# Four layers on one core: a block transpose on VectorE, value products in one series, four column groups, and a normalisation that waits

## The chip, the core and the metric

The kernel runs on one core of a Trainium2 chip. TensorE (PE) multiplies, VectorE (DVE), ScalarE (ACT) and GpSimd (POOL) work element by element, SyncE (SP) issues the DMAs. The metric is the device time of one execution in microseconds. In the profile, PEld is TensorE's weight load and PEclk the clock that TensorE was granted, as a share of full speed.

## The reference

Four sub-layers act on `x` (1024 positions, width 1024, fp32). Each one normalises, mixes, gates and projects back:

```python
h = rmsnorm(x, norm_g[i]) * (1.0 + scale) + shift          # scale, shift, gate = c @ ada_w[i] + ada_b[i]
# i = 0, 3: HGRN2, 8 heads of 128
q, f_pre, i_, z = jnp.split(h @ w_in, 4, axis=-1)           # in outline
f = lb + (1 - lb) * sigmoid(f_pre); k = (1 - lb) * sigmoid(-f_pre); q = silu(q)
S_t = f_t * S_{t-1} + k_t v_t^T;  o_t = q_t S_t             # chunkwise in the code
y = (rmsnorm(o, onorm_g) * silu(z)) @ w_out
# i = 1: 16 query heads of 64 over 4 key heads, window of 128, sinks, rotary, q and k normalised per head
s = einsum(q, k over this block of 128 and the one before) * 64 ** -0.5
y = (softmax with sink(s masked) @ v * silu(z)) @ w_out
# i = 2: gated DeltaNet, 16 value heads of 128 over 8 key heads, causal convolution of 4 taps on q, k, v
X = triangular_solve(A + eye, rhs, unit_diagonal=True)      # per chunk; then a scan over the chunks
y = (rmsnorm(o, onorm_g) * silu(z)) @ w_out
x = x + gate * y
```

## The kernel before

The 1024 positions are worked in two halves of `HT` = 512. Every fp32 projection is split into a high and a low part and done as three products of 128x512 per 128 rows of the contraction (`mm3`, L204 to L206). A weight tile comes by DMA into `w_raw` (L177), ACT rounds it to `w_hi` (L179), DVE subtracts to `w_lo` (L180).

One program order is given by the Python text, and a scheduler turns it into one instruction list per engine by priorities. `weave` steps several generators together by the costs they yield and their totals; `high_priority`, `early` and `burst` (4000) move what is issued inside them forward; `tied` is a burst whose later products may not be parted from the first. Each engine then runs its own list in order, so an instruction that waits holds up all that is behind it on that engine.

*Normalisation* (`norm_apply`, L496 to L506): for each of 8 slices of 128 rows, DVE makes `n_t`, ACT makes `hhi`, DVE makes `hlo`. At the end of a layer both halves of the next layer's input are made there.

*HGRN2* (`hgrn2`, layers 0 and 3): eight heads. While head h is mixed (`mix`), the next head's projections run beside it as filler. In `mix`, levels of growing size fill an attention matrix: each level builds operands `hg_X` (L1061 to L1065, ACT and DVE) and multiplies 32-wide column groups of TensorE (L1040); the last level (L1087) has 12 products of 96, 64 and 32 columns in three column groups. At the end of a head's half, `o_ps` is normalised into `hg_tmp` (L1132), four TensorE transposes turn it into `ot_ps` (L1136), DVE multiplies by the gate `hg_zs` (L1139), and seven of eight heads store to `od` in DRAM.

*Attention* (`swa`, layer 1): K and V of half 0 early, then of half 1, then queries and gates. In `mix`, per block of 128 queries: scores, softmax, then for each of two key blocks four transposes (`pt_ps`, L1368), an ACT copy (`sw_pth`) and two products with the values (`pv_ps`, L1374), the second block's added to the first's.

*Gated DeltaNet* (`gdn`, layer 2): a convolution's eviction takes `gd_xs` (L644) and `gd_tb` (L648) from `proj_ps` on ACT and adds three taps on DVE (L650); `inverse` solves the triangles in steps whose products `z_ps` (L828 among them) are evicted by ACT and DVE. The DVE block transpose (`gd_of`, L859) is already used there, on 128x512 as 32x32 blocks, with stores to `od` of 64 KB (L862).

Of the kernel before, what the change touches and what calls it, by code (L numbers as in the profile page):

```python
# [20 lines left out]
P = 128  # L21
# [9 lines left out]
NB = {"n_acc": 1, "n_sq": 2, "n_t": 2}  # L31
# [52 lines left out]
class Trunk:  # L84
    def __init__(self, ctx, tc, ins):
# [11 lines left out]
        self.od = [self.dram.tile([D * (1 + n), T], F32, name=f"od{n}") for n in range(2)]  # L97
        self.zd = self.dram.tile([2 * D, T], F32, name="zd")
        self.hhi, self.hlo = [None, None], [None, None]
        self.x = [None, None]  # L100
        self.oo, self.pre = {}, {}
# [364 lines left out]
    def norm(self, i, hf):  # L466
        self.norm_apply(i, hf, self.norm_stats(hf))

# [27 lines left out]
    def norm_apply(self, i, hf, rb):  # L496
        nc = self.nc
        x = self.x[hf]
        self.hhi[hf], self.hlo[hf] = self.hslot("hhi"), self.hslot("hlo")
        hhi, hlo = self.hhi[hf], self.hlo[hf]  # L500
        for k in range(KT):
            t = self.np.tile([P, HT], F32, name="n_t", tag="n_t", bufs=NB["n_t"])
            G, S = self.gcol[:, i, k:k + 1], self.shift(i, k)
            nc.vector.scalar_tensor_tensor(t, x[:, k, :], G, rb, ALU.mult, ALU.mult)
            nc.scalar.activation(hhi[:, k, :], t, AF.Identity, bias=S)
            nc.vector.scalar_tensor_tensor(hlo[:, k, :], t, S, hhi[:, k, :].bitcast(F32), ALU.add, ALU.subtract)  # L506

# [29 lines left out]
    def gdn(self, i, side):  # L537
# [98 lines left out]
        def conv(dd, hf, ps, ct, out):  # L636
# [12 lines left out]
            for j in (2, 1, 0):  # L649
                nc.vector.scalar_tensor_tensor(y, xs[:, j:j + HT], w(j), y, ALU.mult, ALU.add)  # L650
# [81 lines left out]
        def inverse(u, dd):  # L732
# [79 lines left out]
            nc.scalar.copy(Z[R[1], :, 0:32], za[R[1]])  # L812
            nc.vector.tensor_copy(Z[R[3], :, 0:32], zb[R[3]])
# [8 lines left out]
            nc.scalar.copy(Z[R[1], :, 0:32], za[R[1]])  # L822
            nc.vector.tensor_copy(uv[R[2], :, R[3]], zb[R[2]])
            nc.vector.tensor_copy(uv[R[0], :, R[1]], za[R[0]])
# [7 lines left out]
            nc.scalar.copy(Z[up, 0:8], z[up])  # L832
            nc.vector.tensor_copy(Z[up, 8:16], z[lo])
# [4 lines left out]
            nc.scalar.copy(uv[lo, 0:8, up], z[lo])  # L838
            nc.vector.tensor_copy(uv[lo, 8:16, up], z[up])
# [25 lines left out]
        def scan(u, dd):  # L865
# [3 lines left out]
            for n in range(C):  # L869
# [50 lines left out]
        self.early(proj_kq(0, ds[0], ((0,),)), EV)  # L920
# [4 lines left out]
              (chain(proj_z(0, ds[0], (1,)), proj_v(0, ds[0]), proj_z(1, ds[1]), proj_kq(1, ds[1])), 72800, 0, 1, 0))  # L925
# [30 lines left out]
    def hgrn2(self, i, side):  # L956
# [7 lines left out]
        bufs = {"X": 1, "q": 3, "f": 3, "kg": 3, "qf": 3, "tmp": 3, "v": 3, "zs": 3, "kht": 1, "k0": 2}  # L964
# [60 lines left out]

        def mix(h, d, halves=(0, 1)):
            S = d.get("S")
            for hf in halves:
# [22 lines left out]
                for l in (1, 3, 5):  # L1051
# [9 lines left out]
                    nc.scalar.copy(xv[:, :, 0:3, :], qv[:, :, 1:4, :])  # L1061
                    nc.vector.tensor_tensor(xv[:, :, 3:5, :], qv[:, :, 2:4, :], bc(1, 3, 2), ALU.mult)
                    nc.vector.tensor_tensor(xv[:, :, nx - 1, :], xv[:, :, 4, :], bc(1, 2, 1)[:, :, 0, :], ALU.mult)
# [14 lines left out]
                    else:  # L1078
# [4 lines left out]
                        with self.burst():  # L1083
                          for c in range(NC):
                            for g in range(3):
                                gs = slice(g * 32, (g + 1) * 32)
                                nc.tensor.matmul(pl[gs, c, g + 1:, :], kg[:, c * P + g * 32:c * P + (g + 1) * 32], xv[:, c, g::3 if g == 0 else 4 - g, :][:, :3 - g, :] if g < 2 else xv[:, c, 2:3, :], start=True, stop=True)  # L1087
                        for g in range(3):
                            gs = slice(g * 32, (g + 1) * 32)
                            nc.scalar.copy(at[gs, :, (g + 1) * 32:], pl[gs, :, g + 1:, :].rearrange("p c b t -> p c (b t)"))  # L1090
                        yield 900
                    for b in (2, 1):
# [17 lines left out]
                sqj = tl("tmp")  # L1110
                for c in range(NC):
# [15 lines left out]
                    nc.scalar.activation(sqj[:, cs], po[:, cs], AF.Square, accum_out=ssq[:, c:c + 1])  # L1127
# [3 lines left out]
                on = tl("tmp")  # L1131
                nc.vector.tensor_tensor(on.rearrange("p (c t) -> p c t", c=NC), po.rearrange("p (c t) -> p c t", c=NC), r[:, :, None].to_broadcast([P, NC, P]), ALU.mult)  # L1132
                pt = self.psum("tr", "ot_ps", 1)
                for c in range(NC):
                    cs = slice(c * P, (c + 1) * P)
                    nc.tensor.transpose(pt[:, cs], on[:, cs], self.ident)  # L1136
                yield 436
                of = tl("tmp")
                nc.vector.tensor_tensor(of, pt, d["zs", hf], ALU.mult)  # L1139
# [10 lines left out]
        ds = [dict() for _ in range(H)]  # L1150
        gv = proj_v(0)
# [67 lines left out]
    def swa(self, i, side):  # L1219
# [33 lines left out]
        def rotate(tp, ps, cg, sg, out):  # L1253
# [7 lines left out]
            nc.vector.tensor_tensor(b4[:, :, :, 32:64], p4[:, :, :, 0:32], bc(sg, slice(32, 64)), ALU.mult)  # L1261
            nc.vector.tensor_tensor(out, a, b, ALU.add)

# [228 lines left out]
```

## Time and profile before

| | |
|---|---|
| runs shown | 2697.25, 2688.8, 2688.89 us; median 2688.89 us |
| profiled execution | 2695.95 us, span 2694.2 us, mean granted clock 0.992 |
| stages, from the start | setup 0 to 76, HGRN2 to 640, attention to 1115, gated DeltaNet to 2130, HGRN2 to the end |
| busy share | PE 97%, PEld 78%, DVE 75%, ACT 47%, POOL 5% |
| chain that ended last | PE 71%, DVE 17%, DMA 5%, ACT 3% |

The busy time of an engine says how full it is over the whole span. A wait of TensorE is listed with the tile and the line that waited, then the engine, tile and line that released it. In the timeline, an instruction's start to the next one's start is what it cost, since matmuls overlap at their ends and the durations shown overlap too.

### The profile page before, as it was taken

The page shows a single profiled execution, that of the slowest core. Times are in us where ns is not written, and L with a number is a line of the kernel's source. Part 1 is how long each engine was busy: PE and PEld are TensorE (multiplying, and loading weights), DVE is VectorE, ACT ScalarE, POOL GpSimd, SP SyncE. Part 2 cuts the span into 40 slices and gives each one's busy share as a digit, 9 for nine tenths or more (in the row PEclk, how much of TensorE's full clock was granted, in tenths as well). Part 3 has the DMA queues.
Part 4 walks back from the last instruction along what each step waited for, and adds up shares of the span by engine and source line. Part 5 has one row for each costly group of instructions (what it writes and reads, how often), then busy time and mean ns, then how long its engine had stood idle before and what let it go on. Part 6 is the DMA issues. An engine that isn't in the chain of part 4 may idle for free.

```text
span 2694.2 us, 51458 instructions
## 1 busy us (share of the span) xinstructions
PE 2609.7 (97%) x18927; PEld 2102.4 (78%) x18927; DVE 2010.2 (75%) x5619; ACT 1272.9 (47%) x3268; POOL 136.7 (5%) x352
## 2 busy tenths in 40 slices
PE   8999999999999999999999999999999999999998
PEld 4878878778878777677877777777788878787877
DVE  6776766788687877777988888989876766656575
ACT  4333333444454655454556556666644433333342
POOL 0000100000000000001001101100000000000000
PEclk9999999999999999999999999999999999999999
DMA  6332222344223252333343333333584221111133
GB/s 241 92 93 84 68 79 72 110 137 157 59 87 103 75 158 91 114 98 84 102 115 99 96 105 100 94 97 82 179 254 132 71 60 37 56 51 43 49 118 115
DMA packets 361490, 273.29 MB, mean 101 GB/s; under 512 B 70499, under 2 KB 294166, under 8 KB 361238
## 3 DMA queue, kind: packets, MB, share of 16 engines
q1 hardware_dynamic: 360950, 268.96, 33.9%
q8 instruction: 149, 2.44, 0.4%
q14 instruction: 103, 0.84, 0.1%
q0 software_dynamic: 288, 1.05, 0.1%
HBM read 224.77 MB, written 45.15 MB: 100 GB/s over the span
## 4 chain that ended last, share of the span: by engine, by line
PE 71%; DVE 17%; DMA 5%; ACT 3%; issue 3%; SPq 1%; POOL 0%; DVEq 0%; ACTq 0%; POOLq 0%
PE proj_ps L206 10%; PE proj_ps L205 9%; PE proj_ps L204 9%; PE outp_ps L204 5%; PE outp_ps L205 5%; PE outp_ps L206 5%; DMA ada_w<-in_ada_w_dram 3%; PE projt_ps L204 3%; PE projt_ps L206 3%; PE projt_ps L205 3%; DVE w_lo L180 2%; DVE gd_tb L650 2%; PE pv_ps L1374 1%; DVE ada_acc L413 1%; PE w_ps L890 1%
## 5 line engine op out<-in xcount | busy, mean ns | idle before, releaser
L204 PE MATMUL proj_ps<-hhi,w_hi 128*128 128x512 f32 x1664 | 675.8, 406 | 6.1 <-ACT gd_tb L648 5.9
L206 PE MATMUL proj_ps<-hhi,w_lo 128*128 128x512 f32 x1664 | 679.9, 409 | 0.0
L205 PE MATMUL proj_ps<-hlo,w_hi 128*128 128x512 f32 x1664 | 671.2, 403 | 0.0
L204 PEld LDWEIGHTS proj_ps<-hhi,w_hi 128*128 128x128 f32 x1664 | 315.3, 190 | 59.4 <-ACT gd_tb L648 6.3
L205 PEld LDWEIGHTS proj_ps<-hlo,w_hi 128*128 128x128 f32 x1664 | 314.7, 189 | 59.0 <-issue 2.4
L206 PEld LDWEIGHTS proj_ps<-hhi,w_lo 128*128 128x128 f32 x1664 | 315.0, 189 | 56.1 <-issue 1.0
L179 ACT CAST w_hi<-w_raw 128x512 fp32r<-128x512 f32 x332 | 202.0, 611 | 303.3 <-PE proj_ps L205 188.1
L180 DVE TENSOR_TENSOR w_lo<-w_raw,w_hi 128x512 fp32r<-128x512 f32 x332 | 223.1, 674 | 155.2 <-ACT w_hi L179 129.1
L205 PE MATMUL projt_ps<-w_lo,hhi 128*128 128x256 f32 x896 | 258.7, 291 | 4.7 <-DVE w_lo L180 4.7
L204 PE MATMUL projt_ps<-w_hi,hhi 128*128 128x256 f32 x896 | 257.8, 290 | 0.6 <-ACT w_hi L179 0.6
L206 PE MATMUL projt_ps<-w_hi,hlo 128*128 128x256 f32 x896 | 256.8, 290 | 0.0
L204 PE MATMUL outp_ps<-o_hi,w_hi 128*128 128x512 f32 x576 | 229.2, 400 | 4.7 <-ACT o_hi L1200 3.4
L205 PE MATMUL outp_ps<-o_lo,w_hi 128*128 128x512 f32 x576 | 229.4, 399 | 0.0
L206 PE MATMUL outp_ps<-o_hi,w_lo 128*128 128x512 f32 x576 | 226.8, 396 | 0.7 <-DVE w_lo L183 0.7
L205 PEld LDWEIGHTS projt_ps<-w_lo,hhi 128*128 128x128 f32 x896 | 171.1, 192 | 8.1 <-DVE w_lo L180 6.0
L204 PEld LDWEIGHTS projt_ps<-w_hi,hhi 128*128 128x128 f32 x896 | 171.1, 192 | 3.7 <-ACT w_hi L179 1.0
L206 PEld LDWEIGHTS projt_ps<-w_hi,hlo 128*128 128x128 f32 x896 | 170.8, 192 | 2.4 <-issue 1.0
L650 DVE SCALAR_TENSOR_TENSOR gd_tb<-gd_xs,taps,gd_tb 128x512 f32<-128x512 f32 x192 | 145.2, 756 | 28.3 <-ACT gd_tb L648 19.7
L182 ACT ACTIVATE w_hi<-w_raw,par 128x512 fp32r<-128x512 f32 (+1 forms) x136 | 94.3, 698 | 137.0 <-PE outp_ps L205 89.2
L204 PEld LDWEIGHTS outp_ps<-o_hi,w_hi 128*128 128x128 f32 x576 | 108.8, 189 | 29.1 <-ACT o_hi L1200 4.9
L413 DVE SCALAR_TENSOR_TENSOR ada_acc<-ada_w,par,ada_acc 128x512 f32<-128x512 f32 x140 | 104.8, 749 | 33.4 <-DMA ada_w<-in_ada_w_dram 32.5
L206 PEld LDWEIGHTS outp_ps<-o_hi,w_lo 128*128 128x128 f32 x576 | 108.7, 189 | 23.5 <-DVE w_lo L183 1.3
(398 smaller groups left out, 4894.8 us busy)
## 6 DMA issues: line engine op xcount, KB each, us to landing
ada_w<-in_ada_w_dram SPq DMA_DIRECT2D x160, 256.0 KB, 2.8
w_raw<-in_hg_in_w_dram SPq DMA_DIRECT2D x136, 256.0 KB, 2.8
w_raw<-in_gd_in_w_dram SPq DMA_DIRECT2D x108, 256.0 KB, 3.0
o_in<-od SPq DMA_DIRECT2D x72, 256.0 KB, 3.2
w_raw<-in_gd_out_w_dram SPq DMA_DIRECT2D x64, 256.0 KB, 2.9
w_raw<-in_sw_in_w_dram SPq DMA_DIRECT2D x48, 256.0 KB, 2.9
w_raw<-in_hg_out_w_dram SPq DMA_DIRECT2D x40, 256.0 KB, 2.8
ada_w<-in_ada_w_dram SPq DMA_DIRECT2D x8, 1024.0 KB, 9.2
```

What stands on the lines that cost most here:

```text
L179: nc.scalar.copy(hi, raw)
L180: nc.vector.tensor_tensor(lo, raw, hi.bitcast(F32), ALU.subtract)
L182: nc.scalar.activation(hi, raw, AF.Copy, scale=scale)
L204: mm(out, a[0], b[0], start=start, stop=False)
L205: mm(out, a[0], b[1], start=False, stop=False)
L206: mm(out, a[1], b[0], start=False, stop=stop)
L413: self.nc.vector.scalar_tensor_tensor(acc, w, c, acc, ALU.mult, ALU.add)
L650: nc.vector.scalar_tensor_tensor(y, xs[:, j:j + HT], w(j), y, ALU.mult, ALU.add)
L890: nc.tensor.matmul(po[:, hd[a]], dd["u"][a, hf][:, cs], rhs, start=True, stop=True)
L1374: nc.tensor.matmul(po[a * 64:(a + 1) * 64], vg[:, n + 1 - nkb + b, :], p4[:, :, a, :], start=b == 0, stop=b == nkb - 1)
```

## The change

1. `norm_apply` is a generator over its 8 slices, with `n_t` in PSUM. The second half's normalisation of the next layer is kept in `self.last`. HGRN2 and attention drain it at their start; gated DeltaNet takes four slices after each convolution's last tap, with `proj_z(1)` of half 0 now in the early part, and the total of the first weave goes from 72800 to 62400.
2. In `inverse`, evictions of z are in `burst`; in HGRN2, the operands `hg_X` too.
3. HGRN2's last level is 16 products of 32, 64, 64 and 32 columns in four column groups, `tied`; ACT copies four pieces instead of three.
4. For heads 0 to 6 of HGRN2, the TensorE transposes go. DVE normalises in a permuted order and transposes 32x32 blocks; four DMAs store to `pd` in DRAM in the transposed order. `gate()`, called in the next half-mix at level 3, loads `pd` back, multiplies with the gate in place and stores to `od`. `zs` has four buffers, not three. Head 7 stays as it was.
5. Attention's entry is V of half 0 and the first two tiles of queries early, then V of half 1, K of all positions (pairs share one reciprocal root), gates, the other queries.
6. Attention's four products with the values are one tied series after both copies.

```diff
-            t = self.np.tile([P, HT], F32, name="n_t", tag="n_t", bufs=NB["n_t"])
+            t = self.psum("lev", "n_t", 2)
...
-                nc.vector.scalar_tensor_tensor(y, xs[:, j:j + HT], w(j), y, ALU.mult, ALU.add)
+                last = nc.vector.scalar_tensor_tensor(y, xs[:, j:j + HT], w(j), y, ALU.mult, ALU.add)
+
+            with self.tc.issue_after(last.ins):
+                drain(take(self.last, self.parts))
...
-            nc.scalar.copy(Z[up, 0:8], z[up])
-            nc.vector.tensor_copy(Z[up, 8:16], z[lo])
+            with self.burst():
+                nc.scalar.copy(Z[up, 0:8], z[up])
+                nc.vector.tensor_copy(Z[up, 8:16], z[lo])
...
-        self.early(proj_kq(0, ds[0], ((0,),)), EV)
+        self.parts = 4
+        self.early(chain(proj_kq(0, ds[0], ((0,),)), proj_z(1, ds[1], (0,))), EV)
+        drain(self.last)
...
+        def gate():
+
+            h, hf, z = pend.pop()
+            rows = (slice(h * P, (h + 1) * P), slice(hf * HT, (hf + 1) * HT))
+            t = tl("tmp")
+            nc.sync.dma_start(t, self.pd[rows])
+            nc.vector.tensor_tensor(v4(z, "c b"), v4(t, "b c"), v4(z, "c b"), ALU.mult)
+            nc.sync.dma_start(od[rows], z)
...
+                        self.tied([lambda c=c, m=m: mm(c, *m) for c in range(NC) for m in (
+                            (0, 3, slice(6, 7), slice(3, 4)), (0, 0, slice(0, 4, 3), slice(1, 3)),
+                            (1, 1, slice(1, 5, 3), slice(2, 4)), (2, 2, slice(2, 3), slice(3, 4)))])
...
+                    if l == 3 and pend:
+                        gate()
...
                 if h < HA:
-                    nc.sync.dma_start(od[h * P:(h + 1) * P, hf * HT:(hf + 1) * HT], of)
+
+
+                    nc.vector.tensor_tensor(v4(on, "b c"), v4(po, "c b"), r[:, :, None, None].to_broadcast([P, NC, 4, 32]), ALU.mult)
+                    ob = tl("tmp")
+                    nc.vector.transpose(ob, on)
+                    dst = self.pd[h * P:(h + 1) * P, hf * HT:(hf + 1) * HT].rearrange("(b q) (a t) -> a q b t", b=4, a=4)
+                    for a in range(4):
+                        nc.sync.dma_start(dst[a], ob[a * 32:(a + 1) * 32].rearrange("q (b t) -> q b t", b=4))
+                    pend.append((h, hf, d["zs", hf]))
...
-                    p4 = ph.rearrange("p (m a t) -> p m a t", m=2, a=2)
-                    for a in range(2):
-                        nc.tensor.matmul(po[a * 64:(a + 1) * 64], vg[:, n + 1 - nkb + b, :], p4[:, :, a, :], start=b == 0, stop=b == nkb - 1)
-                        yield 430
+                    p4s.append(ph.rearrange("p (m a t) -> p m a t", m=2, a=2))
+
+                self.tied([lambda b=b, a=a: nc.tensor.matmul(po[a * 64:(a + 1) * 64], vg[:, n + 1 - nkb + b, :], p4s[b][:, :, a, :], start=b == nkb - 1, stop=b == 0)
+                           for b in reversed(range(nkb)) for a in range(2)])
...
-        self.early(kv(0))
+        def proj_v(hf):
+            return self.proj_tm(self.load_tm(w_in, 1280), ev_v, (2 * hf, 2 * hf + 1))
+
+        ds = [dict(q=[None, None], zs=[None, None], rq=[None, None]) for _ in range(G)]
+        drain(self.last)
+        self.early(chain(proj_v(0), proj_q(0, ds[0], (0, 1))))
         self.spill_x(1)
-        drain(kv(1))
-        ds = [dict() for _ in range(G)]
-        drain(proj(0, ds[0]))
+        drain(proj_v(1))
+        drain(self.proj_tm(self.load_tm(w_in, 1024), ev_k))
+        drain(chain(proj_z(0, ds[0]), proj_q(0, ds[0], (2, 3))))
```

Lines of the changed kernel are numbered a little higher, so L505 becomes L504 and L1374 becomes L1416. ACT's list at the entry of gated DeltaNet, before (`hhi` is the second half's normalised input, `gd_xs` and `gd_tb` the first convolution's eviction):

```order
L505 ACTIVATE hhi<-n_t,mod 128x512
L179 CAST w_hi<-w_raw 128x512
L505 ACTIVATE hhi<-n_t,mod 128x512 x2
L179 CAST w_hi<-w_raw 128x512
L505 ACTIVATE hhi<-n_t,mod 128x512 x2
L644 COPY gd_xs<-proj_ps 128x512
L648 ACTIVATE gd_tb<-proj_ps,taps 128x512
```

The same place after the change:

```order
L480 ACTIVATE n_sq<-x_11341 128x512
L180 CAST w_hi<-w_raw 128x512
L644 COPY gd_xs<-proj_ps 128x512
L648 ACTIVATE gd_tb<-proj_ps,taps 128x512
L555 CAST gd_wab<-w_raw 128x8x32
L644 COPY gd_xs<-proj_ps 128x512
L180 CAST w_hi<-w_raw 128x512 x2
L654 ACTIVATE gd_tb<-gd_tb 128x512
L504 ACTIVATE hhi<-n_t,mod 128x512 x2
```

The first convolution's two evictions now stand ahead of the second half's `hhi`.

TensorE's list in attention's mix, before (`pv_ps` are products with the values, `projt_ps` the filler's projections):

```order
L204 MATMUL projt_ps<-w_hi,hhi 128x256
L205 MATMUL projt_ps<-w_lo,hhi 128x256
L1374 MATMUL pv_ps<-sw_pth,v 64x256 x2
L1368 MATMUL pt_ps<-ident,sw_sm 128x128 x4
L1330 MATMUL qt_ps<-ident,sw_q 64x128
L206 MATMUL projt_ps<-w_hi,hlo 128x256
L1330 MATMUL qt_ps<-ident,sw_q 64x128 x2
L204 MATMUL projt_ps<-w_hi,hhi 128x256
L1330 MATMUL qt_ps<-ident,sw_q 64x128
L1374 MATMUL pv_ps<-sw_pth,v 64x256 x2
```

After:

```order
L207 MATMUL projt_ps<-w_hi,hlo 128x256
L205 MATMUL projt_ps<-w_hi,hhi 128x256
L206 MATMUL projt_ps<-w_lo,hhi 128x256
L1416 MATMUL pv_ps<-sw_pth,v 64x256 x4
L207 MATMUL projt_ps<-w_hi,hlo 128x256
L205 MATMUL projt_ps<-w_hi,hhi 128x256
```

Two series of two became one of four; over the layer, 57 series (54 of two products, 3 of four) became 32 (28 of four, 4 of two).

VectorE's list at the end of a head's half in the last HGRN2 layer, before:

```order
L1132 TENSOR_TENSOR hg_tmp<-o_ps,rs_y 128x512
L976 TENSOR_TENSOR hg_q<-proj_ps,hg_tmp 128x16x32
L180 TENSOR_TENSOR w_lo<-w_raw,w_hi 128x512
L1139 TENSOR_TENSOR hg_tmp<-ot_ps,hg_zs 128x512
L1124 SCALAR_TENSOR_TENSOR hg_S<-hg_S,hg_F,s_ps 128x128 x3
```

After (L1159 normalises, L1044 is the gate of the stretch loaded back from `pd`):

```order
L1159 TENSOR_TENSOR hg_tmp<-o_ps,rs_y 128x4x4x32
L1149 SCALAR_TENSOR_TENSOR hg_S<-hg_S,hg_F,s_ps 128x128
L1161 STREAM_TRANSPOSE hg_tmp<-hg_tmp 128x512
L985 TENSOR_TENSOR hg_q<-proj_ps,hg_tmp 128x16x32
L181 TENSOR_TENSOR w_lo<-w_raw,w_hi 128x512
L993 TENSOR_SCALAR hg_f<-hg_f,omlb,lb 128x512
L1003 TENSOR_TENSOR hg_q<-hg_q,hg_f 128x16x16
L994 TENSOR_SCALAR hg_k_25748<-hg_k_25748,omlb 128x512
L1004 TENSOR_TENSOR hg_qf<-hg_q,hg_f 128x256
L998 TENSOR_TENSOR hg_kg<-hg_k_25748,hg_f 128x256
L1005 TENSOR_TENSOR hg_qf<-hg_q,hg_f 128x256
L1044 TENSOR_TENSOR hg_zs<-hg_tmp,hg_zs 128x512
```

Here eight instructions of VectorE stand between the transpose and the gate; this is one of 14 places of 28 where the two are near, and at the other 14 there are some tens.

## Rows read from the trace of the kernel before

**Rows 1.** The page, part 1: busy time, share of the span, instructions of each engine.

```profile
PE 2609.7 (97%) x18927; PEld 2102.4 (78%) x18927; DVE 2010.2 (75%) x5619; ACT 1272.9 (47%) x3268; POOL 136.7 (5%) x352
```

**Rows 2.** Stretches: length, busy PE, PEld, DVE, ACT, POOL, then clock, DMA share, GB/s.

```profile
76.00:527.00 451.00, 437.73 (x4159) 361.48 (x4157) 313.81 (x1011) 157.09 (x381) 30.81 (x65) 1.00 0.29 85
635.00:708.00 73.00, 67.01 (x523) 63.93 (x523) 55.24 (x144) 28.09 (x54) 0.00 (x0) 0.98 0.37 123
1113.00:1172.00 59.00, 50.44 (x218) 37.22 (x216) 42.81 (x91) 26.17 (x59) 3.03 (x11) 0.94 0.38 112
```

**Rows 3.** What TensorE waited for: total us, times, longest us.

```profile
PE z_ps L828 <- DVE gd_uq L823: 6.6, 7, 1.6
PE proj_ps L204 <- ACT gd_tb L648: 5.9, 1, 5.9
PE ot_ps L1136 <- DVE hg_tmp L1132: 5.6, 11, 1.3
PE projt_ps L205 <- DVE w_lo L180: 4.7, 5, 1.4
PE ab_ps L575 <- DVE gd_tb L727: 2.0, 1, 2.0
```

**Rows 4.** Groups by line: busy us, mean ns of one, idle before.

```profile
L1136 PE MATMUL ot_ps<-ident,hg_tmp 128*128 128x128 f32 x128 | 20.8, 280 | 5.9 <-DVE hg_tmp L1132 5.6
L859 DVE STREAM_TRANSPOSE gd_of<-gd_of 128x512 f32<-128x512 f32 x32 | 22.5, 704 | 0.1
```

**Rows 5.** TensorE in order of time, a head transpose: start us, us, instruction.

```profile
127.67 0.66 PE L1136 MATMUL ot_ps<-ident,hg_tmp 128*128 128x128 f32 x4
128.16 0.39 PE L1114 MATMUL o_ps<-hg_S,hg_qf 128*128 128x128 f32 x2
```

**Rows 6.** TensorE in order of time, value products, a long and a short series.

```profile
742.67 0.40 PE L206 MATMUL proj_ps<-hhi,w_lo 128*128 128x512 f32 x1
742.91 0.39 PE L204 MATMUL proj_ps<-hhi,w_hi 128*128 128x512 f32 x1
743.23 1.08 PE L1374 MATMUL pv_ps<-sw_pth,v 128*64 128x256 f32 x8
744.25 0.50 PE L205 MATMUL proj_ps<-hlo,w_hi 128*128 128x512 f32 x1
...
765.03 0.65 PE L1374 MATMUL pv_ps<-sw_pth,v 128*64 128x256 f32 x4
765.62 0.66 PE L1368 MATMUL pt_ps<-ident,sw_sm 128*128 128x128 f32 x4
```

**Rows 7.** TensorE in order of time, a lower level and the last level.

```profile
153.92 0.55 PE L1040 MATMUL lev_ps<-hg_X,hg_kg 128*32 128x48 f32 x32 [0.28 <-DVE hg_X L1063]
154.39 0.50 PE L206 MATMUL proj_ps<-hhi,w_lo 128*128 128x512 f32 x1
...
157.34 0.85 PE L1087 MATMUL lev_ps<-hg_X,hg_kg 128*32 128x96 f32 x24
158.12 0.50 PE L206 MATMUL proj_ps<-hhi,w_lo 128*128 128x512 f32 x1
```

**Rows 8.** Busy time by stretch at the start of gated DeltaNet.

```profile
1131.00:1138.00 7.00, 1.14 (x4) 0.62 (x4) 7.00 (x11) 5.18 (x9) 1.27 (x4) 0.75 0.38 97
1138.00:1142.00 4.00, 3.90 (x14) 2.67 (x12) 2.71 (x5) 0.88 (x3) 1.47 (x6) 0.59 0.39 98
```

**Rows 9.** DMA: the issue on its queue (ns), KB, median us to landing.

```profile
L862 SPq DMA_DIRECT2D od<-gd_of x128: 302/432/1777, 1305.2 to 1986.0; - x128
...
od<-gd_of SPq DMA_DIRECT2D x128, 64.0 KB, 1.8
o_in<-od SPq DMA_DIRECT2D x72, 256.0 KB, 3.2
```

**Rows 10.** VectorE in 76 to 527 us, then what the DMA queue waited for.

```profile
L413 DVE SCALAR_TENSOR_TENSOR ada_acc<-ada_w,par,ada_acc 128x512 f32<-128x512 f32 x56 | 41.9, 748 | 23.2 <-DMA ada_w<-in_ada_w_dram 22.9
...
SPq L427 <- DVE w_lo L180: 127.2, 47, 9.6
```

More of the change, by code (lines that the diff above doesn't have):

```diff
@@ L100, in __init__ @@
         self.x = [None, None]
-        self.oo, self.pre = {}, {}
+        self.oo, self.pre, self.last, self.parts = {}, {}, iter(()), 0
     def hslot(self, name):
@@ L837, in inverse @@
                        for n in range(8) for g, q in ((n + 8, up), (n, lo))])
-            nc.scalar.copy(uv[lo, 0:8, up], z[lo])
-            nc.vector.tensor_copy(uv[lo, 8:16, up], z[up])
+            with self.burst():
+                nc.scalar.copy(uv[lo, 0:8, up], z[lo])
+                nc.vector.tensor_copy(uv[lo, 8:16, up], z[up])
             yield 900
@@ L1082, in mix, with mm @@
                         pl = self.psum("lev", "lev_ps", 2).rearrange("p (c b t) -> p c b t", c=NC, t=32)
[L1083 to L1090, printed above, removed]
+                        def mm(c, k, g, x, b):
+                            return nc.tensor.matmul(pl[g * 32:(g + 1) * 32, c, b], kg[:, c * P + k * 32:c * P + (k + 1) * 32], xv[:, c, x, :], start=True, stop=True)
+                        self.tied([lambda c=c, m=m: mm(c, *m) for c in range(NC) for m in (
+                            (0, 3, slice(6, 7), slice(3, 4)), (0, 0, slice(0, 4, 3), slice(1, 3)),
+                            (1, 1, slice(1, 5, 3), slice(2, 4)), (2, 2, slice(2, 3), slice(3, 4)))])
+                        for k, g, b0, b1 in ((0, 0, 1, 3), (1, 1, 2, 4), (2, 2, 3, 4), (0, 3, 3, 4)):
+                            nc.scalar.copy(at[k * 32:(k + 1) * 32, :, b0 * 32:b1 * 32], pl[g * 32:(g + 1) * 32, :, b0:b1, :].rearrange("p c b t -> p c (b t)"))
                         yield 900
+                    if l == 3 and pend:
+                        gate()
                     for b in (2, 1):
@@ L1261, in rotate @@
             nc.vector.tensor_tensor(b4[:, :, :, 32:64], p4[:, :, :, 0:32], bc(sg, slice(32, 64)), ALU.mult)
+            out = a if out is None else out
             nc.vector.tensor_tensor(out, a, b, ALU.add)
+            return out
         def sumsq(ps, out):
@@ L1278, in ev_k @@
[L1278 to L1286 removed]
+            if tp % 2 == 0:
+                ks["ms"] = sp.tile([P, 16], F32, name="k_ms", tag="k_ms", bufs=1)
@@ new lines, in ev_k @@
+            sumsq(ps, ks["ms"][:, (tp % 2) * 8:(tp % 2) * 8 + 8])
+            ks[tp % 2] = rotate(tp, ps, cgk, sgk)
+            if tp % 2 == 0:
+                return
+            nc.vector.tensor_scalar(ks["ms"], ks["ms"], 1.0 / 64, EPS, ALU.mult, ALU.add)
+            r = self.rsqrt(ks["ms"], 16, "q", sp)
+            for n in range(2):
+                kr = ks[n].rearrange("p (a d) -> p a d", d=64)
+                nc.vector.tensor_tensor(kr, kr, r[:, n * 8:n * 8 + 8, None].to_broadcast([P, 8, 64]), ALU.mult)
+                for t2 in range(2):
+                    pt = self.psum("tr", "kt_ps", 1)
+                    for h in range(4):
+                        nc.tensor.transpose(pt[:64, h * P:(h + 1) * P], kr[:, t2 * 4 + h, :], self.ident)
+                    t0 = 2 * (tp - 1 + n) + t2
+                    ts = slice(t0 * P, (t0 + 1) * P)
+                    p4 = pt.rearrange("p (h t) -> p h t", h=4)
+                    for dst, src in ((k012[:, :3, ts], p4[:64, :3]), (k3[:, ts], p4[:64, 3])):
+                        nc.scalar.copy(dst[:64], src)
+                        nc.vector.tensor_tensor(dst[64:], src, dst[:64].bitcast(F32), ALU.subtract)
@@ L1434, in trunk @@
                 k.preload(hg_in_w[0], (x,))
-        k.norm_apply(layers[0], 0, rb)
-        rb = k.norm_stats(1, k.load_x(sp, 1))
-        k.norm_apply(layers[0], 1, rb)
+        drain(k.norm_apply(layers[0], 0, rb))
+        k.last = k.norm_apply(layers[0], 1, k.norm_stats(1, k.load_x(sp, 1)))
+        drain(k.last)
         if layers[0] % 3:
@@ L1457, in trunk @@
                     k.open_norm()
-                k.norm(nxt, hf)
-                if nxt % 3 and hf == 0:
-                    k.spill_x(0)
-                if hf == 1:
+                a = k.norm_apply(nxt, hf, k.norm_stats(hf))
+                if hf == 0:
+                    drain(a)
+                    if nxt % 3:
+                        k.spill_x(0)
+                else:
+                    k.last = a
                     k.nst.close()
```

87 lines of the change are left out of this document (37 added, 50 removed).

## The prediction

> **What bounds the kernel now.** I read the page's busy shares first: TensorE is busy for 97% of the span, VectorE for 75%, ScalarE for 47% [rows 1]. So a microsecond is won where TensorE is given less to do, or where one of its few waits goes; work moved to VectorE or ScalarE is free as long as it does not make TensorE wait. Next the stretches: in the first HGRN2 layer, 76 to 527 us, TensorE shows 437.73 of 451 us, VectorE 313.81 (70%), ScalarE 157.09; in attention's entry, 635 to 708, TensorE shows 67.01 of 73; around the entry of gated DeltaNet 50.44 of 59 [rows 2]. The two entries are where idle time is concentrated. Then the list of what TensorE waited for, which names the places: z products 6.6 us in 7 waits, one wait of 5.9 us at a convolution's eviction, `ot_ps` 5.6, attention's `w_lo` 4.7, `ab_ps` 2.0 [rows 3]. Last the timeline, for what a series costs from its start to the next start.
>
> **Head transposes (part 4).** Four transposes start at 127.67 and the next instruction at 128.16: 0.49 us a series [rows 5]. Seven heads, two halves and two layers make 28 series: 28 x 0.49 = 13.7 us off TensorE. The group has 128 transposes, 32 series, and waited 5.6 us in 11 waits for `hg_tmp` [rows 3, 4]; 28/32 of it, 4.9 us, goes too. What is late next is the next head's work behind the same VectorE chain, so I take half of the wait as returning: 13.7 + 2.45 = 16.2 us; bounds 10 (all waits return, and some more) and 18.6.
>
> What is added: 28 block transposes of 0.704 us on VectorE [rows 4], 19.7 us, over two layers in each of which VectorE is idle for 137 of 451 us [rows 2]; they lie beside TensorE's projections. Without that cover they would be 19.7 us. The gate's multiplication only moves. Each gate waits for a DMA chain: four stores issued 0.432 us apart, landing after 1.8 us, and a load of 256 KB like `o_in`, 3.2 us [rows 9]: 3 x 0.43 + 1.8 + 3.2 = 6.3 us. On VectorE's list 14 of the 28 gates have only 3 to 10 instructions (mean 6.3) between transpose and gate. At the mean duration of 2010.2/5619 = 0.36 us [rows 1] that is 2.3 us of work, at 70% busy 3.2 us of time. So VectorE can stand 6.3 - 3.2 = 3.1 us at each, and behind it stand the evictions of filler projections, operands of the next level and `w_lo`. TensorE feels this only where its buffers run out. The nearest row for a TensorE wait on a VectorE chain at this place is `ot_ps`, 5.6/11 = 0.51 us [rows 3]; I charge it to seven of the 14: -3.6 us. Bounds 0 and 14 x 3.1 = -43 us. The fourth `zs` buffer costs nothing. The other 14 have 30 or more instructions, some 11 us of work, and cover the chain.
>
> **Value products in one series (part 6).** A series of two products (four records) takes 0.59 us from 765.03 to 765.62, one of four 1.02, from 743.23 to 744.25; the projection product before a series takes 0.32 us to the next start, where 0.24 is usual [rows 6]. Two short series against one long: 2 x 0.59 - 1.02 + 0.08 = 0.24 us. 25 series fewer give 6.0 us. Bounds 0 (the long series waits for the later of two copies, and no other work stands ready) and 8.
>
> **Last level in four groups (part 3).** The old one takes 0.78 us (157.34 to 158.12): its busiest column group passes 4 x 96 = 384 columns. A lower level with 16 products of 48 columns, 192 in each group, takes 0.47 (153.92 to 154.39) [rows 7]. The new busiest group has 256: 0.47 + 64/192 x 0.31 = 0.57, so 0.21 us each, and 2 layers x 16 half-heads give 32: 6.6 us. ScalarE's fourth copy is 32 times its mean of 1272.9/3268 = 0.39 us [rows 1], 12.5 us beside 157 us busy of 451 [rows 2]; it would show only if TensorE waited for `at`. The rule of the Trainium skill that speaks against it is in "TensorEngine Tiling (Array Packing)", section Instruction Overhead: every product carries about 60 cycles, and tiling should not be taken from a dimension that is already small. By it 32 records instead of 24 would not be cheaper; the trace bears it out little, since 32 records at the lower level took less than 24 here [rows 7].
>
> **Entry of gated DeltaNet (parts 1 and 2).** TensorE shows 1.14 us of work in the 7 us from 1131, and in the next 4 the granted clock is 0.59, near its lower level [rows 8]. The wait is for a convolution's eviction on ScalarE, which stood behind the second half's `hhi`. With it ahead, 5.9 goes, and of the lower clock (1 - 0.59) x 4 = 1.6 us, and the 2.0 of `ab_ps` [rows 3]: 9.5; the normalisation must still be finished before the second half's projections, so 1.0 returns: 8.5, bounds 4 and 9.5. `n_t` in PSUM I price at nothing, since ScalarE and VectorE, which read it, are below 75% busy; the levels' two PSUM buffers that it takes have no other user in that stretch. Bounds: one wait like that of `ab_ps`, 2 us, either way.
>
> **Attention's entry (part 5).** Of 73 us TensorE is idle in 6.0 [rows 2], 4.7 of it in five waits for `w_lo` [rows 3]; at clock 0.98 a lower clock costs 73 x 0.02 = 1.5. The new order starts with projections that need fewer VectorE instructions for each product, but the same weights have to be loaded. I take half of 7.5, 3.7; bounds -2 and 6.
>
> **Inverse's evictions (part 2).** Seven waits, 6.6 us in all [rows 3]. Bursting moves the eviction forward, but TensorE's filler between two series shrinks too. I take 2, bounds -3 and 6.6. The HGRN2 operands in `burst` I take at nothing, since projections lie between the levels; the wait that the row of a level shows is 0.28 us [rows 7], so over 32 half-heads 9 us either way bounds it.
>
> **Sum.** 16.2 - 3.6 + 6.0 + 6.6 + 8.5 + 3.7 + 2.0 = 39.4 us. The profiled execution took 2695.95 us, so 2656.6; it was 7.06 us above the median of the runs shown, 2688.89, so 2649.5, or 2650 us.
>
> **Rivals.**
>
> *The waits come back elsewhere.* TensorE at 97% runs so close to its operands that what is taken off one wait is found at the next. For it: all terms that are waits (2.45 + 8.5 + 3.7 + 2.0 = 16.7) and half of the value products' (3) do not come. Against it: the two entries' waits are long and single. 2650 + 20 = 2670 us.
>
> *Slower: the gate's round trip through DRAM stops VectorE.* SP issues in order, and weight loads there wait for `w_lo` buffers: 127.2 us in 47 waits, 2.7 us each, at L427's issue alone [rows 10]. If the load of `pd` stands behind one such wait, the chain is 9.0 us and VectorE stands 9.0 - 3.2 = 5.8 us at 14 gates; if TensorE loses all of it, 81 us, against the other terms' 43.0: 38 us slower, 2727. It decides from 43.0/14 = 3.1 us lost per near gate. For it: the weights need VectorE themselves (`w_lo`), so VectorE and SP can hold up each other. Against it: TensorE has projections in front of it whose operands are already there, and VectorE already stands 23.2 us at `ada_acc` waiting for a DMA in this layer [rows 10], and TensorE is busy all the same.
>
> *The last level goes by the number of its products.* 24 records in 0.78 us would be 32 in 1.04: +0.26 x 32 = 8.3 us instead of -6.6, so 2650 + 15 = 2665 us. The page named above would have it so. Against it: 32 records in 0.47 [rows 7].
>
> *All comes in full.* 18.6 + 8 + 6.6 + 9.5 + 6 + 6.6 and no loss at the gates: 55.3, or 2633.6 us: 2634. For it: each wait removed here had the eviction order as its only cause. Against it: the first rival.
>
> **How the numbers follow.** Forecast 0.55, with its own range of 2638 to 2662; waits come back 0.20; slower 0.07; the last level by number 0.03; all in full 0.15. A difference of 0.3%, 8 us, is about what a measurement of this kernel can tell from no change, so faster means below 2681 and slower above 2697. The first rival, with the gates at twice their price, reaches the zone of no change: 0.06 from it and from a milder second rival. Slower 0.08, faster 0.86. The range that leaves out the slower case, the outer part of the best and the worst of the first rival is 2626 to 2680.
>
> **What would show it.** After: `ot_ps` left with 16 transposes; the wait of 5.9 us at the entry gone and no clock below 0.9 behind it; the last level at 0.55 to 0.6 us; value products mainly in series of 1.02 us; VectorE waiting for the DMA of `pd` at 14 gates for some 3 us each, and TensorE waiting little behind it. The prediction is wrong if TensorE's waits on VectorE in the HGRN2 layers rise by more than some 10 us, if these layers' stretches do not shrink by some 10 us each, or if the attention layer, with series waiting for two copies, does not get shorter.

## The result, and the profile after

The changed kernel is slower by a hair: 2696.62 us median of 22 runs against 2691.15, a ratio of 1.0023 (interval 1.0017 to 1.003). The forecast was 2650. Its profiled execution took 2701.0 us at a mean clock of 0.986; before it was 0.992.

The page's busy times of the kernel after [against rows 1]:

```profile
PE 2597.5 (96%) x19071; PEld 2102.0 (78%) x19071; DVE 2022.1 (75%) x5629; ACT 1274.2 (47%) x3304; POOL 139.4 (5%) x352
```

TensorE is busy for 12 us less over a span that is 5 us longer, and part of the busy time is at the lower clock. So work did leave TensorE, and time came back. The two series whose durations were forecast came out as forecast; the timeline of TensorE after, a last level and a series of four value products (start us, us, instruction):

```profile
205.11 0.65 PE L1107 MATMUL lev_ps<-hg_X,hg_kg 128*32 128x32 f32 x32
205.69 0.39 PE L206 MATMUL projt_ps<-w_lo,hhi 128*128 128x256 f32 x1
...
773.08 1.08 PE L1416 MATMUL pv_ps<-sw_pth,v 128*64 128x256 f32 x8
774.10 0.28 PE L1387 MATMUL s_ps<-band,identb 128*128 128x256 bf16 x1
```

The last level takes 205.69 - 205.11 = 0.58 us (0.78 in [rows 7], forecast 0.57), the long series 1.02 like that of [rows 6]. The waits of TensorE after (total us, times, longest):

```profile
PE lev_ps L1061 <- DVE hg_X L1085: 8.2, 17, 1.6
PE proj_ps L207 <- DVE w_lo L181: 6.3, 2, 4.1
PE outp_ps L207 <- DVE w_lo L184: 5.2, 2, 4.1
...
PE o_ps L1139 <- DVE hg_tmp L1159: 3.7, 10, 1.1
...
PE z_ps L833 <- DVE gd_uq L828: 3.2, 3, 1.5
...
PE z_ps L824 <- issue: 2.0, 2, 1.8
...
PE proj_ps L205 <- ACT gd_tb L648: 1.5, 1, 1.5
```

Against [rows 3]: the wait of 5.9 for `gd_tb` is 1.5, and 6.3 for `w_lo` stands in its place; 5.6 for `ot_ps` went, and `o_ps` waits 3.7 for the same VectorE chain, where it waited 1.7 before; a new 4.1 for `w_lo` stands at the output projection of the first HGRN2 layer. At the entry of gated DeltaNet the timeline of VectorE, and of TensorE's product that waits, shows why (after):

```profile
1138.28 1.40 DVE L505 SCALAR_TENSOR_TENSOR hlo<-n_t,mod,hhi 128x512 fp32r<-128x512 f32 x2
1139.60 1.40 DVE L503 SCALAR_TENSOR_TENSOR n_t<-x,gcol,n_rb 128x512 f32<-128x512 f32 x2
1141.40 0.69 DVE L730 SCALAR_TENSOR_TENSOR gd_tb<-gd_tb,proj_ps 128x512 f32<-128x512 f32 x1 [0.40 <-ACT gd_tb L729]
1142.00 1.40 DVE L505 SCALAR_TENSOR_TENSOR hlo<-n_t,mod,hhi 128x512 fp32r<-128x512 f32 x2
1143.32 1.88 DVE L181 TENSOR_TENSOR w_lo<-w_raw,w_hi 128x512 fp32r<-128x512 f32 x3
1144.06 0.52 PE L207 MATMUL proj_ps<-hhi,w_lo 128*128 128x512 f32 x1 [4.13 <-DVE w_lo L181]
```

VectorE works through four slices of the second half's normalisation after the convolution, and the `w_lo` that TensorE needs is behind them. The same work now blocks another operand. The granted clock then falls to 0.57, so the sign "no clock below 0.9 behind it" failed (busy PE, PEld, DVE, ACT, POOL, granted clock, DMA share, GB/s):

```profile
1144.00:1148.00 4.00, 3.94 (x10) 3.16 (x11) 1.40 (x4) 0.62 (x1) 0.00 (x0) 0.57 0.66 187
```

Two of the signs of a wrong prediction came too. In the last HGRN2 layer the stretch from the first level product to the first output product shrank from 436.6 to 433.0 us, and not by some 10. The attention layer, from its first `qt_ps` to gated DeltaNet's first `ab_ps`, takes 434.9 us after 435.5.

The other part is the clock. Two stretches of 100 us of gated DeltaNet and the start of its output, first before, then after (same columns):

```profile
1222.00:1322.00 100.00, 97.36 (x652) 78.33 (x650) 76.04 (x210) 49.90 (x159) 7.49 (x18) 0.95 0.37 98
...
1422.00:1522.00 100.00, 98.17 (x688) 79.06 (x687) 88.10 (x253) 59.84 (x190) 9.57 (x24) 1.00 0.40 104
...
1922.00:1960.00 38.00, 35.20 (x161) 27.97 (x161) 32.21 (x76) 23.57 (x68) 0.00 (x0) 0.96 0.68 211
```

```profile
1222.00:1322.00 100.00, 96.78 (x677) 77.89 (x675) 85.41 (x246) 56.38 (x177) 6.89 (x18) 1.00 0.39 105
...
1422.00:1522.00 100.00, 98.01 (x665) 78.69 (x664) 85.26 (x242) 55.42 (x176) 7.72 (x21) 0.95 0.37 96
...
1922.00:1960.00 38.00, 32.72 (x166) 25.37 (x167) 27.63 (x60) 22.37 (x65) 0.00 (x0) 0.87 0.66 203
```

The lower level (half of full speed) stands in other places and is met more often: over the 22 runs of the changed kernel the mean clock is 0.9873; for the kernel before it is 0.9928 to 0.9934 in the 17 to 35 runs that stand beside the experiments below. In the run after, projection products of 128x512 start 0.23 us apart at 1138 us and 0.43 at 1145. Time x (1 - mean clock) is then an estimate of what the lower level costs, and an upper one, since it takes all the time there to be so slowed: over the 22 runs the time rises by 20 us for each 0.01 of clock lost, where the estimate would have 27. By it the changed kernel loses 34 us and the kernel before 18 to 19; the rest of the time is some 10 us shorter after. So the removed work shows, and the lower clock took more than that.

### The profile page after: what moved, and what is told of

The parts are those of the page before. It is cut to its first block, busy times and chain, and to the rows that moved or that the text cites. A ratio compares the mean times of both kernels' runs of the same rounds, so it can differ in the third digit from the quotient of the medians.

```text
span 2699.3 us, 52029 instructions
## 1 busy us (share of the span) xinstructions
PE 2597.5 (96%) x19071; PEld 2102.0 (78%) x19071; DVE 2022.1 (75%) x5629; ACT 1274.2 (47%) x3304; POOL 139.4 (5%) x352
## 4 chain that ended last, share of the span: by engine, by line
PE 67%; DVE 18%; DMA 6%; ACT 4%; issue 3%; SPq 1%; POOL 0%; DVEq 0%; ACTq 0%
PE proj_ps L207 8%; PE proj_ps L206 8%; PE proj_ps L205 8%; PE outp_ps L206 5%; PE outp_ps L205 4%; PE outp_ps L207 4%; PE projt_ps L205 3%; PE projt_ps L206 3%; PE projt_ps L207 3%; DMA ada_w<-in_ada_w_dram 2%; DVE w_lo L181 2%; DVE gd_tb L650 2%; PE pv_ps L1416 1%; PE ada_row L401 1%; PE w_ps L897 1%
## 5 line engine op out<-in xcount | busy, mean ns | idle before, releaser
L206 PEld LDWEIGHTS outp_ps<-o_lo,w_hi 128*128 128x128 f32 x576 | 110.0, 191 | 27.4 <-DVE o_lo L1234 5.0
```

The lines of the kernel that those rows point to most:

```text
L206: mm(out, a[0], b[1], start=False, stop=False)
```

## The experiments

First each part alone on the kernel before, with its lines of the change as shown ahead. The kernel before is run beside each on the same chip; its medians were 2691 to 2693 us. Stretches and waits come from one profiled execution each. Where an edit leaves the first HGRN2 layer as it was, the stretch from its first level product to its first output product still varies from 445 to 450 us; in the last HGRN2 layer such runs agree within 0.4 us.

**Head transposes alone (part 4).**

```diff
-                    nc.tensor.transpose(pt[:, cs], on[:, cs], self.ident)
+                    nc.vector.transpose(ob, on)
```

> The kernel before with part 4 alone: block transpose on VectorE, round trip through pd, gate later. Theory 1 (the work that leaves TensorE does leave the span, and the loss of the whole change sits in the parts that only move instructions): 12 us faster, about 2679, with the HGRN2 stretches some 6 us shorter each and TensorE's idle time up by under 4 us. Theory 2 (TensorE runs so close to its operands that work taken off it returns as waits and as stretches at the lower clock): within 3 us of before, with idle time up by 8 us or more. My rival of a stalled VectorE: slower by 10 us or more.

2693.89 us, ratio 1.001 (1.0 to 1.002): nothing gained. From the first level product to the first output product the HGRN2 layers became 2.3 and 3.8 us shorter; of these only the 3.8 of the last layer are clear of the spread. TensorE's waits in this run:

```profile
PE lev_ps L1053 <- DVE hg_X L1076: 10.1, 18, 1.9
PE o_ps L1129 <- DVE hg_tmp L1149: 4.7, 11, 1.3
PE o_ps L1130 <- POOL hg_at L1094: 2.2, 1, 2.2
...
PE z_ps L829 <- issue: 2.1, 1, 2.1
...
PE z_ps L822 <- issue: 1.5, 2, 0.8
```

The 4.9 us of `ot_ps` waits come back in full, on `o_ps` (1.7 before), `hg_X` (6.8 before) and `hg_at` (none before). And z products of gated DeltaNet, a layer whose instruction lists this part leaves as they were, stall for 3.6 us with nothing that the profile names, where the kernel before has 0.3; from its first `ab_ps` to its first output product this layer takes 790.1 us, where the kernel before takes 785.4. All listed waits of TensorE sum to 84 us, against 75 before. The stalls are taken up below. My rival of a stalled VectorE is out: the loss is under 10 us, and in the whole change no wait of TensorE over 0.15 us stands within 8 us behind any of the nine gates that waited for `pd`. VectorE's wait for `pd` in the whole change, and the block transpose's group:

```profile
DVE hg_zs L1044 <- DMA hg_tmp<-pd: 6.0, 9, 1.6
```

```profile
L1161 DVE STREAM_TRANSPOSE hg_tmp<-hg_tmp 128x512 f32<-128x512 f32 x28 | 19.8, 706 | 0.2
```

**Value products alone (part 6).**

```diff
+                self.tied([lambda b=b, a=a: nc.tensor.matmul(...)
+                           for b in reversed(range(nkb)) for a in range(2)])
```

> The kernel before with part 6 alone: the products with the values of both key blocks in one series. Theory 1: 6 us faster, all of it in the attention stretch. Theory 2: within 2 us, because the long series waits for two copies; the waits of pv_ps and qt_ps rise and the attention stretch has more of the lower clock.

2694.27 us, ratio 1.0013 (1.0003 to 1.0022). The busy time of TensorE's value products fell from 38.5 to 33.0 us, the stretch of mixing, from the first `qt_ps` to the first output product, from 276.3 to 273.7; runs that leave it as it was have 274.4 to 277.0. The waits of the attention layer, 700 to 1110 us, in this run:

```profile
PE qt_ps L1330 <- DVE mod L439: 4.5, 2, 4.1
PE s_ps L1345 <- ACT sw_sm L1357: 2.4, 3, 1.9
PE pt_ps L1368 <- ACT sw_pth L1371: 1.3, 4, 0.7
```

The wait of `qt_ps` was 1.2 us before. It is not one for an operand: `qt_ps` takes the one buffer of the PSUM tag `tr`, which `ada_ps`, the modulation of the next layer, holds until VectorE has read it into `mod`:

```profile
972.28 0.31 PE L435 MATMUL ada_ps<-ada_red,eye 128*128 128x48 f32 x2
976.22 0.36 DVE L439 TENSOR_TENSOR mod<-ada_ps,adab 32x12 f32<-32x12 f32 x2
976.72 1.03 PE L1330 MATMUL qt_ps<-ident,sw_q 128*64 128x128 f32 x4 [4.13 <-DVE mod L439]
```

The mean clock is lower too, 0.9918 over 12 runs against 0.9934, some 4 us by the estimate above. Theory 2 is the nearer one: the lower clock came, but of the waits that it named only `qt_ps` rose by more than 1 us, and not because of the two copies.

**Attention's entry alone (part 5).**

```diff
-        self.early(kv(0))
+        self.early(chain(proj_v(0), proj_q(0, ds[0], (0, 1))))
```

> The kernel before with part 5 alone: attention's entry in the new order. Theory 1: 3 to 6 us slower, since in the whole change entry and mix together became 1 us shorter while the value products alone should have given 6. Theory 2, by which the forecast of 3.7 us faster held and was eaten elsewhere: 2 to 4 us faster.

2686.88 us, ratio 0.9986 (0.9975 to 0.9998): 3.8 us, as the prediction had it. Theory 1 falls here. In 597 to 717 us TensorE waits 1.5 us for `w_lo`, where it waited 4.2 before.

**The inverse's bursts alone (part 2)**, and only those of the 64-wide products.

```diff
+            with self.burst():
+                nc.scalar.copy(Z[up, 0:8], z[up])
+                nc.vector.tensor_copy(Z[up, 8:16], z[lo])
```

> The kernel before with the bursts on the evictions in the inverse alone (of part 2). Theory 1: slower by 5 to 10 us, with more stretches at the lower clock in the gated DeltaNet layer, where the whole change has 34 us of them against 17 (1253.9, 1571.4 and 1929.8 before). Theory 2: 0 to 3 us faster, with the waits of z_ps at half or less and as many stretches at the lower clock as before.

> The kernel before with bursts only on the evictions of the 64-wide products in the inverse (the last two steps). Theory 1 (the lower clock comes from z series that follow each other more closely): the time lost to the lower clock, median x (1 - mean clock), is above before's 18 us by 3 to 8, the rest 2 to 4 us shorter; in sum 0 to 4 slower. Theory 2 (the lower clock in this layer comes by chance): both within 2 us of before.

2695.82 us, ratio 1.0017 (1.0007 to 1.0027), at a mean clock of 0.9897 over 12 runs; the 64-wide ones alone 2691.06, ratio 0.9999 (0.9989 to 1.0008), at 0.9909. The waits of `z_ps` in the first of these:

```profile
PE z_ps L830 <- DVE gd_uq L825: 5.1, 4, 1.6
PE z_ps L839 <- DVE gd_Z L836: 2.1, 2, 1.9
PE z_ps L830 <- ACT gd_tb L665: 1.8, 1, 1.8
PE z_ps L830 <- ACT gd_Z L824: 1.4, 1, 1.4
```

That is 10.4 us, where the kernel before has 7.2 on all lines of `z_ps` (6.6 of them in [rows 3]): the waits on evictions did not fall. My reading is that earlier evictions bring the next series earlier, with less of the projections between. But these waits are not what made the kernel slower, since all of TensorE's waits together are 73 us here and 75 before. By the estimate above the lower clock takes 28 us, 10 more than before, and the rest is 5 us shorter; with the 64-wide ones alone it takes 5 more and the rest is 6 shorter, near what theory 1 had. That a shorter distance between z series is what lowers the clock was not shown by itself.

**The normalisation alone (part 1)**, and with `n_t` of the first half back in SBUF.

```diff
-            t = self.psum("lev", "n_t", 2)
+            t = self.psum("lev", "n_t", 2) if hf else self.np.tile([P, HT], F32, name="n_t", tag="n_t", bufs=2)
```

> The kernel before with part 1 alone: the second half's normalisation left over, n_t in PSUM, the new early part and total in gated DeltaNet. Theory 1 (the parts that only move instructions bring the loss): the wait of 5.9 us at the entry goes, but the first weave starts later and other waits come; within 3 us of before or up to 8 us slower. Theory 2 (the forecast held here): 8 us faster.

> Part 1 alone as before, but n_t of the first half stays in SBUF (two buffers); only the second half's is in PSUM. Theory 1 (n_t takes the two PSUM buffers that the last head's second half and attention's second half of scores need, so these can no longer run ahead of the first half's normalisation): lev_ps of the last head is back before 530 us, the stretches around both layers' ends lose their 13 us, and the kernel is 10 us faster than part 1 alone, about 2693 or less. Theory 2 (the loss is the later entry and the waits for w_lo): still 8 us or more slower than before.

Alone 2704.21 us, ratio 1.0042 (1.0028 to 1.0055), the costliest part, and slower than either theory had it; with the line above 2692.54, ratio 1.0001 (0.9991 to 1.0011): 11 us back. By the estimate above, 7 to 8 of them are time at the lower clock. The level products (`lev_ps` alone, same columns as above, without POOL) in two stretches at the end of the first HGRN2 layer, before, part 1 alone, and with `n_t` in SBUF:

```profile
490.00:530.00 40.00, 4.54 (x240) 3.65 (x240) 4.05 (x16) 2.17 (x6) 0.96 0.37 109
590.00:615.00 25.00, 0.00 (x0) 0.00 (x0) 0.00 (x0) 0.00 (x0) 1.00 0.32 93
```

```profile
490.00:530.00 40.00, 2.28 (x120) 1.83 (x120) 2.04 (x8) 1.09 (x3) 0.96 0.38 113
590.00:615.00 25.00, 3.02 (x120) 2.51 (x120) 1.93 (x8) 1.09 (x3) 0.93 0.26 73
```

```profile
490.00:530.00 40.00, 4.54 (x240) 3.65 (x240) 4.01 (x16) 2.18 (x6) 0.97 0.36 108
590.00:615.00 25.00, 0.00 (x0) 0.00 (x0) 0.00 (x0) 0.00 (x0) 1.00 0.31 91
```

The last head's second half has 120 records of level products. Before, they stand beside the first half's; with `n_t` in the same two PSUM buffers they come 100 us later, since in program order the first half's normalisation takes these buffers first. Attention's scores use the same buffers; there only the last block of queries moves, with its `qt_ps` 16 us behind those of the block before instead of 5. Of the causes that were taken out one by one, this is the largest.

**The last level alone (part 3).**

```diff
-                            for g in range(3):
+                        self.tied([lambda c=c, m=m: mm(c, *m) for c in range(NC) for m in (
```

> The kernel before with the last level of HGRN2 alone in four column groups (part 3). Theory 1: 6 us faster, 0.78 to 0.58 us in each of 32 series. Theory 2: within 2 us, the time back as waits for hg_X or hg_at.

2684.64 us, ratio 0.9972 (0.996 to 0.9984): 7.5 us. From the first level product to the first output product the two layers are 3.6 and 3.5 us shorter.

**The operands' burst alone (part 2).**

```diff
+                    with self.burst():
+                        nc.scalar.copy(xv[:, :, 0:3, :], qv[:, :, 1:4, :])
```

> The kernel before with the burst on the operands hg_X alone (of part 2). Theory 1: between 3 us faster and 6 us slower, as an order that moves VectorE's w_lo and evictions back. Theory 2: no change within 2 us.

2693.04 us, ratio 1.0001 (0.9992 to 1.0009).

**Parts 3 and 5 together.**

> The kernel before with parts 3 and 5 alone, the two that were faster by themselves. If effects add: 8 + 4 = 12 us faster than before, about 2680. If what one frees the other's order takes back: 6 us or less.

2686.38 us, ratio 0.9987 (0.9974 to 1.0). The two do not add. The profiled execution, 8 us over the median, shows a part of the reason: in the last HGRN2 layer TensorE waits 5.7 us in three waits for GpSimd's copies into `hg_at`, which it does not do with part 3 alone. These copies, 0.45 us in the median, took up to 3.3 us there; why is open.

**The whole change, mended in steps.** Without the inverse's bursts:

```diff
-            with self.burst():
-                nc.scalar.copy(Z[up, 0:8], z[up])
+            nc.scalar.copy(Z[up, 0:8], z[up])
```

> The whole change without the bursts on the evictions in the inverse. Theory 1: 5 to 10 us faster than the whole change, about 2689, with fewer stretches at the lower clock in gated DeltaNet. Theory 2: within 3 us of the whole change, about 2697, or 2 us slower.

2696.02 us, ratio 1.0013 (1.0002 to 1.0023): the same as the whole change within the intervals. With `n_t` of the first half in SBUF instead (the line above), then also without the transposes' part, without the bursts, and with two slices:

```diff
-        self.parts = 4
+        self.parts = 2
```

> The whole change with n_t of the first half in SBUF. Theory 1: 8 to 12 us faster than the whole change, 2685 to 2689. Theory 2: within 3 us of the whole change, 2697.

> The whole change with n_t of the first half in SBUF, and with the head transposes left on TensorE as before. Theory 1 (the transposes bring what the HGRN2 stretches show, 6 us): about 2692, 6 us slower than with them (2686). Theory 2 (as alone, they bring nothing): 2684 to 2688.

> The whole change with n_t of the first half in SBUF, without the bursts in the inverse. Theory 1 (the bursts shorten the rest by 6 us and cost 8 at the lower clock): time lost to the lower clock 19 instead of 27 us, the rest 6 us longer, in sum 2682 to 2686. Theory 2 (the lower clock has other causes): lost time as before, 2690 or more.

> The whole change with n_t of the first half in SBUF, and two slices of the second half's normalisation after each convolution instead of four. Theory 1 (the wait of 4 us for w_lo at gated DeltaNet's entry stands behind the four slices on VectorE): that wait falls by half and 2 to 4 us go, about 2683. Theory 2: the slices only stand elsewhere, within 2 us of 2686.

2685.99 us, ratio 0.9976 (0.9966 to 0.9985), so 11 us faster than the whole change. Without the transposes' part 2688.33, ratio 0.9988 (0.9978 to 0.9997): it brings 2 to 3 us there, not 6, and the intervals overlap. Without the bursts 2686.96, ratio 0.9988 (0.9975 to 1.0001), at a mean clock of 0.9919 against 0.9898: by the estimate above the lower clock takes 22 us, not 27, and the rest is 6 us longer, so there is no difference in time. With two slices 2677.55, ratio 0.9952 (0.9933 to 0.997). The entry's waits there, 1105 to 1180 us:

```profile
PE proj_ps L205 <- ACT gd_tb L648: 1.5, 1, 1.5
PE proj_ps L207 <- DVE w_lo L181: 0.8, 1, 0.8
```

The 6.3 us for `w_lo`, which stand in the run with four slices too, are 0.8, and the stretch from attention's first output product to gated DeltaNet's first scan products is 8 us shorter. That is more than the wait itself; of the 8 us that the kernel gained in all, some 4 are time at the lower clock by the estimate above.

**Place in TensorE's stream.** Transposes of the identity whose results nobody reads, ahead of the first layer; n is 56 on part 4 alone, 8 on the kernel before, and 56 on the mended change with two slices.

```diff
+        pt = self.psum("tr", "pad_ps", 1)
+        for n in range(56):
+            nc.tensor.transpose(pt[:, n % 4 * P:(n % 4 + 1) * P], self.ident, self.ident)
```

> Part 4 alone, and 56 transposes of the identity before the first layer (as many as part 4 takes from the first HGRN2 layer), whose results nobody reads; they cost up to 5 us where TensorE mostly waits for the first DMAs. Theory 1 (what part 4 loses in gated DeltaNet comes from the place of its instructions in TensorE's stream): stalls of z_ps that the profile lists under issue fall from 3.6 us to under 1, and the rest outside the HGRN2 layers is 4 us shorter than in part 4 alone. Theory 2 (the place plays no part): stalls and rest as in part 4 alone.

> The kernel before with 8 transposes of the identity before the first layer, whose results nobody reads. Theory 1 (the place of the z products in TensorE's stream decides whether they stall; the changed kernel's net shift ahead of gated DeltaNet is these 8): stalls of z_ps under issue rise from 0.3 us to about 3 us and the rest is 3 to 5 us longer, about 2695. Theory 2 (chance, or something else in part 4): stalls under 1 us, within 2 us of before.

> The whole change with n_t of the first half in SBUF, two slices after each convolution, and 56 transposes of the identity before the first layer, whose results nobody reads. Theory 1: stalls of z_ps under issue fall from 2.5 us to under 1, 2 to 5 us faster than without the 56, about 2674. Theory 2: within 2 us of 2678, or 3 us slower for the added work.

From 60 us on, the instruction lists of TensorE, VectorE and ScalarE are those of the same kernel without the added work. On part 4 alone: 2688.59 us, ratio 0.9989 (0.9979 to 0.9999), 5 us faster than without the added work, and no stall of `z_ps` under issue is listed, where 3.6 us were. On the kernel before, 8 transposes: the stalls rise, as this row of it shows with one of 0.2 beside, from 0.3 us to 1.6,

```profile
PE z_ps L824 <- issue: 1.4, 1, 1.4
```

but the time does not: 2689.21, ratio 0.9993 (0.9984 to 1.0002). On the mended change: 2669.44 us, ratio 0.9919 (0.9905 to 0.9934), 8 us faster than without, and no such stall. So the added transposes move the stalls, in all three. From its first `ab_ps` to its first output product gated DeltaNet became 4.8 us shorter on part 4 alone (785.3, as before) and 4.5 on the mended change. What a stall costs is not settled: with the 8 transposes this stretch is shorter in spite of its stalls (781.6), and in the mended change two stretches ahead of gated DeltaNet were shorter too (the first HGRN2 layer's mixing by 3.1 us, from there to attention's first key transposes by 3.6). Nor is it shown that it is the place in the stream: the 56 transposes also start the first layer some 1.5 us later. This is the fastest version here, 0.8% ahead of the kernel before. Its busy times:

```profile
PE 2585.3 (97%) x19127; PEld 2094.3 (79%) x19127; DVE 2022.9 (76%) x5629; ACT 1275.2 (48%) x3304; POOL 138.8 (5%) x352
```

## Why the prediction was wrong, step by step

| term | forecast us | alone, ratio x 2691 |
|---|---|---|
| head transposes | -12.6 | +3 |
| value products | -6.0 | +3 |
| last level | -6.6 | -7.5 |
| gated DeltaNet's entry with `n_t` | -8.5 | +11 |
| attention's entry | -3.7 | -4 |
| inverse's bursts | -2.0 | +5 |
| operands' burst | 0 | 0 |

They add up to some +10, the whole change measured +6; my sum was -39.4. The mended kernel with the 56 transposes, at -22, has a little over half of it; where the other 17 us are is open, since the parts do not add.

*The step that failed*, the largest of several, is "`n_t` in PSUM I price at nothing", for the reason that "the levels' two PSUM buffers that it takes have no other user in that stretch". I looked at the stretch of gated DeltaNet alone. The edit stands in a function that every layer runs, and at the end of the HGRN2 and attention layers the other half's mixing wants the same buffers. Runs `norm_sbuf` and `all_sbuf` put this at 11 us, against the 2 that I gave as bounds. This is program order and was there to be read; the 7 to 8 us of it that are lower clock I could not have read off it.

*The entry of gated DeltaNet*: "1.0 returns" was the second. The wait for `gd_tb` went as I said, and 6.3 us for `w_lo` came. I had looked at ScalarE's list, where the eviction moved ahead, and not at VectorE's, where the same slices moved ahead of `w_lo`. Two slices instead of four showed it.

*The head transposes*: the work left, 12.2 us of the forecast 13.7. The series of 0.49 us that I read is among the longest; all 32 take 13.7 us together, 0.43 each. "I take half of the wait as returning" failed, since all of it came back, on the same chain and on `hg_at`. The gates that I charged 3.6 us cost TensorE nothing that could be seen: VectorE waited 6.0 us in 9 places for `pd`, 1.6 at most, where I had 14 times 3.1, and no wait of TensorE follows within 8 us. Of the forecast 12.6 the layers show at most 6.1, and gated DeltaNet became 4.7 longer; the run with 56 transposes put back gave that back.

*The value products and the inverse*: the durations of the series were right, and so was the removal of series. What I had not priced is a wait for a shared PSUM buffer (`qt_ps`, 4.5 us), evictions that keep TensorE waiting as before (`z_ps`), and the lower clock, 4 and 10 us by the estimate above. That the moved work lowers the clock is seen in these runs; by what way is not shown. This is near my first rival, to which I gave 0.20 and 20 us, but that one spoke of waits and not of the clock; with the PSUM buffers on top it was larger.

*Right* was the last level, with its time by the busiest column group and not by the number of its products: 32 records take 0.58 us where 24 took 0.78. The Trainium skill ("TensorEngine Tiling (Array Packing)", section Instruction Overhead) gives every product about 60 cycles; my reading of it, that more products would not be cheaper, did not hold here. Right was attention's entry alone too, with less waiting for `w_lo` as forecast, though half of a sum with bounds of -2 to 6 made that cheap.

## What to carry to other kernels

An edit that gives a tile another pool changes the order of everything that shares the pool: list its users in every layer that runs the function, and in program order, before it is priced at nothing. A wait that goes is worth only the distance to the next operand on the engine that fed it, so read that engine's list behind the moved instruction too. On an engine that is 97% busy, neither removed waits nor removed work could be added up here: of three removals of work the last level's showed in the time, and those of the transposes and value products alone did not. Look at the mean clock beside the time before a removal is called useless: time x (1 - clock) tells how much of the loss may lie there.

## What the runs showed of the hardware

Transposes added ahead of the first layer, whose results nobody reads, made two kernels 5 and 8 us faster and took away stalls of 3.6 and 2.5 us in series of small products that come 1200 to 1900 us later; 8 of them on the kernel before brought stalls of 1.3 us more and changed nothing in the time. The mean granted clock of one program over its runs spreads by 0.003 to 0.007 in the programs that were run 11 times or more (0.986 to 0.991 in the whole change), and time goes with it: 2691.09 us at 0.991, 2703.34 at 0.986.
